# Five unused tiles that move the matmul operands of a two-block network by 64 to 320 bytes in SBUF

## The chip, the cores and the metric

The kernel runs on one core of one Trainium2 chip. The metric is the device time of one execution in microseconds (us); smaller is better. The kernel before takes 2571.19 us, the median of three runs between 2569.83 and 2571.62.

## The reference

Two network blocks run one after the other on a sequence of 512 tokens of width 1024, in fp32.

```
x1 = x + g_a * token_mixer(modulate(rmsnorm(x)), modulate(rmsnorm(ctx)))   # block 1
x2 = x1 + g_f * expert_choice_ffn(modulate(rmsnorm(x1)))                   # 16 experts
x3 = rmsnorm(x2)
h  = x3 + concat(pool_mixer, deltanet)(rmsnorm(x3) @ w_in) @ w_out         # block 2
h  = h + cross_attention(rmsnorm(h), mem)
h  = h + relu(rmsnorm(h) @ w_up)**2 @ w_down
out = rmsnorm(h)
```

The token mixer holds three branches: a gated linear recurrence with 8 heads, a gated convolution of width 3, and attention with 16 query heads. Nearly all the arithmetic is in products of a feature matrix (512 x 1024, or 256 x 1024 for the context) with a weights matrix.

## The kernel before, in words

**A product in three matmuls.** Weights arrive in `raw` tiles of 128 x 8 x 256 values by SyncE's DMA queue (`wload`). ScalarE rounds them into a high part `wh`, and VectorE takes the rest into a low part `wl` (`wsplit`, L111 and L112). Features are held in the same way as a high and a low tile. A product is then high x high, high x low and low x high, three matmuls in the type fp32r for each of the eight blocks of 128 rows. There are two forms:

- `lin_steps` (L120 to L128): the weights are the stationary operand, 128 columns of them, and the features stream past as the moving operand, 512 columns wide (256 for the context, for the memory and in two places that work in halves). L125 and L126 use `wh`, L127 uses `wl`.
- `lin_n` (L139 to L147): the features are the stationary operand, 128 tokens of them, and 256 columns of weights stream past. L145 and L147 stream `wh`, L146 streams `wl`.

```
self.nc.tensor.matmul(ps, a, xa, start=k == 0, stop=False)       # L125: a = weights, xa = features
self.nc.tensor.matmul(ps, xa, a, start=start and k == 0, ...)    # L145: the roles exchanged
```

Each matmul loads its stationary operand anew; the profile counts as many weight loads (PEld) as matmuls.

**Where the tiles lie.** SBUF is shared out by pools that stand like two stacks in each partition: a pool on the left side takes the next addresses upward, one on the right side the next addresses downward, and a release gives them back. `build` (L1424) makes all pools in order. A tile's address is thus the sum of the sizes of what stands before it. `wh` and `wl` stand at the start of the left stack, just above the constants, for the whole program: at 48,416, 56,608, 64,800 and 72,992 bytes, each with the remainder 32 modulo 256. The features stand in these tiles, with their first addresses in the built program:

| tile | holds | product it enters | address | modulo 256 |
|---|---|---|---|---|
| `hx` | normed tokens, block 1 | moving 512 (recurrence, gates, convolution); stationary (values, keys, queries) | 196,576 | 224 |
| `hc` | normed context | moving 256; stationary | 97,568 | 32 |
| `br`, `ao` | a branch's output | moving 512 (`merge`); `br` also stationary (`out_proj`) | 163,808 | 224 |
| `mT` | normed memory | moving 256; stationary (`mem_kv`) | 196,576 | 224 |
| `hn` | normed tokens entering block 2 | moving 512 | 97,568 | 32 |
| `y2`, `xo` | mixer's output, cross attention's output | stationary (`add_lin`) | 97,568 | 32 |
| `hxh`, `hxl` | normed tokens, cross attention and MLP | moving 512 (first group: in halves of 256) | 196,576 | 224 |
| `mh`, `ml` | MLP's hidden units | stationary (second half of `mlp`) | 120,736 | 160 |

In every one of these tiles the slices that matmuls read begin at multiples of 512 bytes from the tile's start, and the slices of `wh` and `wl` do as well, so one remainder holds for all slices of a tile.

**What sets the order.** Instructions are recorded in program order, with a priority for the weights' split, and a wait is put wherever a tile's data or its buffer is not yet there. Each engine takes its instructions in that order. The experts in between (`expert_pair`, L871) stream 201 MB of weights that come straight from memory, in plain fp32, and use no split.

Of the kernel before, what the change touches and what calls it, by code (L numbers as in the profile page):

```python
# [6 lines left out]
FT = mybir.dt.float32  # L7
# [71 lines left out]
class Net:  # L79
# [1344 lines left out]
    def build(self):  # L1424
        tc = self.tc
        P = lambda name, side="right", **kw: tc.alloc_tile_pool(name=name, bufs=1, side=side, reuse_waits="tile", **kw)
# [2 lines left out]

        self.xp = P("aT", "left")  # L1430
        self.aT = self.xp.tile([128, KK, S], FT, name="aT", tag="x")
        self.hcp = P("hctx", "left")
        self.hc = [[self.hcp.tile([128, C], FR, name=f"hc{p}{k}") for k in range(KK)] for p in "hl"]
        self.lpx = P("granule")
        self.lp = P("long")
        hx = [(self.lpx if i == 2 else self.lp).tile([128, 4, S], FR, name="hx", tag=f"hx{i}") for i in range(4)]
# [114 lines left out]
                self.pool_group(hd + 1)  # L1551
        self.hnp.release()
        self.y2p = P("y2", "left")
        self.y2 = self.hl(self.y2p, "y2", S)
        for k in range(4):
            self.split(self.y2[0][k], self.y2[1][k], self.ypool[:, k])
# [12 lines left out]
        self.dump("x3", self.x1)  # L1569
        self.y2p.release()  # L1570
        self.ap = P("cross", "left")
        self.xo = self.hl(self.ap, "xo", S)
        self.cross()
        self.hn = hl2()
# [1 line left out]
        nt.release()  # L1576
        self.ap.release()
        self.dump("x4", self.x1)
        self.ap = P("mlp")
        self.mlp()  # L1580
        self.ap.release()
        self.hnp.release()
        self.pp.release()
        self.xp.release()
        self.wp.release()
# [37 lines left out]
```

## Time and profile before

| | us |
|---|---|
| median of three runs | 2571.19 |
| the profiled execution, in all | 2567.61 |
| its span in the profile | 2565.8 |
| TensorE (PE) busy | 2468.1 |
| VectorE (DVE) busy | 1225.4 |
| ScalarE (ACT) busy | 992.6 |
| mean granted clock of TensorE | 0.992 |

The profile's time of one matmul is not what a matmul costs in a stream: matmuls overlap, and the profile models their ends. A row of the timeline has a start, and the distance between the starts of two matmuls, divided by the number of matmuls from one to the other, is the cost of one in that stream. The rows below are used in that way. [...]

In program order the span holds: norms and modulation (to 50 us), the recurrence's heads (50 to 500), merge, keys, convolution (to 860), queries and attention (to 1130), merge, memory, output projection and routing (to 1270), experts (to 1760), block 2's input products and delta solve (to 2010), its output projection, cross attention and MLP (to the end).

### The profile page before, as it was taken

Reading aid. Unit: us, or ns where it says so; the run is one execution under the profiler, and the core shown is the slowest. Engines: PE = TensorE matmul, PEld = TensorE weight load, DVE = VectorE, ACT = ScalarE, POOL = GpSimd, SP = SyncE. Lnnn points to the kernel's source line nnn. Section 1 sums busy time; section 2 is a strip of 40 time slices with the busy share of each in tenths; the row PEclk is TensorE's granted clock in tenths of the full one; section 3 lists DMA queues with packets and bytes.
Section 4 is the critical chain, followed back from the end, with each engine's and each line's share of the span. In section 5 each row is a group of like instructions: output and inputs, shape, how many; then the busy total and the mean of one; then the engine's idle time right before and its main releaser. Section 6 shows DMA issues by size and latency. Waiting matters only on the chain.

```text
span 2565.8 us, 34426 instructions
## 1 busy us (share of the span) xinstructions
PE 2468.1 (96%) x14348; PEld 1875.9 (73%) x14348; DVE 1225.4 (48%) x1960; ACT 992.6 (39%) x1665; POOL 100.0 (4%) x124
## 2 busy tenths in 40 slices
PE   6999999999999999999999999998999999999998
PEld 4888888689888886679833333334778989889898
DVE  4557575734443565544522222225884464532433
ACT  4446444542233466644321111114664444431332
POOL 0000000000001110010100000000000010000000
PEclk9999999999999999999999999998999999999999
DMA  8233222422323220044899999995220132223321
GB/s 276 66 83 99 83 67 66 140 91 83 99 83 98 84 81 1 1 149 156 295 406 409 409 409 410 409 409 185 66 82 17 34 99 66 91 83 99 99 99 50
DMA packets 244220, 386.85 MB, mean 151 GB/s; under 512 B 6864, under 2 KB 189136, under 8 KB 244064
## 3 DMA queue, kind: packets, MB, share of 16 engines
q1 hardware_dynamic: 238784, 365.98, 40.4%
q0 software_dynamic: 4704, 16.57, 1.8%
q8 instruction: 113, 1.85, 0.3%
q10 hardware_dynamic: 576, 2.10, 0.2%
q14 instruction: 43, 0.35, 0.0%
HBM read 376.23 MB, written 6.29 MB: 149 GB/s over the span
## 4 chain that ended last, share of the span: by engine, by line
PE 83%; DMA 7%; DVE 5%; ACT 4%; issue 1%; POOL 0%; SPq 0%; POOLq 0%; ACTq 0%; DVEq 0%
PE lin L125 11%; PE lin L126 11%; PE lin L127 11%; PE pair L871 11%; PE lin L145 6%; PE lin L147 6%; PE lin L146 6%; DMA ew<-in_w_up 4%; PE oT L717 2%; PE lps L383 2%; PE s L690 2%; DMA ew<-in_w_down 1%; PE ptp L704 1%; PE sps L953 1%; PE dzp L1239 1%
## 5 line engine op out<-in xcount | busy, mean ns | idle before, releaser
L112 DVE TENSOR_TENSOR wl<-raw,wh 128x1024 fp32r<-128x1024 f32 (+1 forms) x262 | 312.3, 1227 | 215.8 <-ACT wh L111 212.8
L111 ACT CAST wh<-raw 128x1024 fp32r<-128x1024 f32 (+1 forms) x262 | 258.5, 1028 | 404.3 <-PE lin L126 251.4
L871 PE MATMUL pair<-ew,XT 128*64 128x512 f32 x1024 | 259.0, 598 | 11.5 <-DMA ew<-in_w_up 11.4
L127 PE MATMUL lin<-hx,wl 128*128 128x512 f32 x576 | 231.4, 402 | 0.0
L125 PE MATMUL lin<-hx,wh 128*128 128x512 f32 x576 | 229.8, 399 | 0.0
L126 PE MATMUL lin<-hx,wh 128*128 128x512 f32 x576 | 227.9, 396 | 0.0
L871 PEld LDWEIGHTS pair<-ew,XT 128*64 128x64 f32 x1024 | 81.4, 136 | 167.0 <-issue 133.3
L145 PE MATMUL lin<-wh,mh 128*128 128x256 f32 x512 | 145.0, 283 | 0.0
L147 PE MATMUL lin<-wh,ml 128*128 128x256 f32 x512 | 144.7, 283 | 0.0
L146 PE MATMUL lin<-wl,mh 128*128 128x256 f32 x512 | 144.0, 281 | 0.0
L871 PE MATMUL pair<-ew,hT 128*64 128x512 f32 x512 | 138.4, 599 | 1.9 <-DMA ew<-in_w_down 1.9
L125 PE MATMUL lin<-hxh,wh 128*128 128x512 f32 (+1 forms) x352 | 131.7, 376 | 1.0 <-ACT hxh L972 0.9
L126 PE MATMUL lin<-hxl,wh 128*128 128x512 f32 (+1 forms) x352 | 131.9, 375 | 0.1
L127 PE MATMUL lin<-hxh,wl 128*128 128x512 f32 (+1 forms) x352 | 131.5, 375 | 0.0
L127 PEld LDWEIGHTS lin<-hx,wl 128*128 128x128 f32 x576 | 108.3, 188 | 25.7 <-issue 1.0
L125 PEld LDWEIGHTS lin<-hx,wh 128*128 128x128 f32 x576 | 108.4, 188 | 24.6 <-issue 1.2
L126 PEld LDWEIGHTS lin<-hx,wh 128*128 128x128 f32 x576 | 108.3, 188 | 24.7 <-issue 0.2
L871 PEld LDWEIGHTS pair<-ew,hT 128*64 128x64 f32 x512 | 44.7, 136 | 76.2 <-issue 67.0
L146 PEld LDWEIGHTS lin<-wl,mh 128*128 128x128 f32 x512 | 96.8, 189 | 0.1
L145 PEld LDWEIGHTS lin<-wh,mh 128*128 128x128 f32 x512 | 96.6, 189 | 0.1
L147 PEld LDWEIGHTS lin<-wh,ml 128*128 128x128 f32 x512 | 96.3, 188 | 0.0
L145 PE MATMUL lin<-wh,hx 128*128 128x256 f32 x320 | 91.2, 285 | 0.4 <-DVE sig L499 0.4
(547 smaller groups left out, 5423.9 us busy)
## 6 DMA issues: line engine op xcount, KB each, us to landing
ew<-in_w_gate SPq DMA_DIRECT2D x64, 1024.0 KB, 19.4
ew<-in_w_up SPq DMA_DIRECT2D x64, 1024.0 KB, 18.6
ew<-in_w_down SPq DMA_DIRECT2D x64, 1024.0 KB, 18.9
raw<-in_w_in SPq DMA_DIRECT2D x34, 1024.0 KB, 5.0
raw<-in_w_in SPq DMA_DIRECT2D x52, 512.0 KB, 5.3
raw<-in_ada_w SPq DMA_DIRECT2D x24, 1024.0 KB, 7.1
raw<-in_w_up SPq DMA_DIRECT2D x16, 1024.0 KB, 5.4
raw<-in_w_down SPq DMA_DIRECT2D x16, 1024.0 KB, 5.0
```

What stands on the lines that cost most here:

```text
L111: nc.scalar.copy(wh[:, a:a + 4, :n], raw[:, a:a + 4, :n])
L112: nc.vector.tensor_sub(wl[:, a:a + 4, :n], raw[:, a:a + 4, :n], wh[:, a:a + 4, :n].bitcast(FT))
L125: self.nc.tensor.matmul(ps, a, xa, start=k == 0, stop=False)
L126: self.nc.tensor.matmul(ps, a, xb, start=False, stop=False)
L127: self.nc.tensor.matmul(ps, b, xa, start=False, stop=k == KK - 1)
L145: self.nc.tensor.matmul(ps, xa, a, start=start and k == 0, stop=False)
L146: self.nc.tensor.matmul(ps, xa, b, start=False, stop=False)
L147: self.nc.tensor.matmul(ps, xb, a, start=False, stop=stop and k == KK - 1)
L383: nc.tensor.matmul(ps[:, c].rearrange("p (b h x) -> p b h x", h=2, x=m), Xc[:, c], Y[:, c * n4:(c + 1) * n4], start=True, stop=True)
L690: nc.tensor.matmul(s[:, a:b], qT[2 * pair + hh][:, 128 * t:128 * t + 128], kT[p][:, a:b], start=p == 0, stop=p == 1)
L717: self.nc.tensor.matmul(self.oT[64 * hh:64 * hh + 64], self.vn[:, kt, 64 * g:64 * g + 64], PT[kt // 2][:, 2 * (kt % 2) + hh], start=kt == ...
L871: self.nc.tensor.matmul(ps[j][64 * e:64 * e + 64], lhs[:, k0 + k, 64 * e:64 * e + 64], w[e][:, k, 512 * j:512 * j + 512], start=k0 + k == ...
```

## The change

Five tiles are allocated that nothing reads or writes: two of 192 bytes a partition, two of 64 and one of 128. Three stand at the bottom of left pools that are later released (`hctx`, `y2` and `cross`), and two have right pools of their own: `gap`, which stands under everything on the right side for the whole program, and `gapm`, under the MLP's pool.

```
         self.hcp = P("hctx", "left")
+        self.hcp.tile([128, 48], FT, name="gap")
         self.hc = [[self.hcp.tile([128, C], FR, name=f"hc{p}{k}") for k in range(KK)] for p in "hl"]
+        gap = P("gap")
+        gap.tile([128, 48], FT, name="gap2")
         self.lpx = P("granule")
...
         self.y2p = P("y2", "left")
+        self.y2p.tile([128, 16], FT, name="gap3")
         self.y2 = self.hl(self.y2p, "y2", S)
...
         self.ap = P("cross", "left")
+        self.ap.tile([128, 16], FT, name="gap4")
         self.xo = self.hl(self.ap, "xo", S)
...
+        gap2 = P("gapm")
+        gap2.tile([128, 32], FT, name="gap5")
         self.ap = P("mlp")
         self.mlp()
         self.ap.release()
+        gap2.release()
         self.hnp.release()
+        gap.release()
```

No engine's instructions change their order, their shapes or their number: the two built programs hold the same 18,012 instructions, and one wait differs (a GpSimd fill of the convolution's padding waits for a matmul three places earlier). What changes is addresses. The weights' tiles and the constants stay. Of the remainders modulo 256:

| tile | before | after | features minus weights, before | after |
|---|---|---|---|---|
| `wh`, `wl` | 32 | 32 | | |
| `hx`, `br`, `ao`, `mT`, `hxh`, `hxl` | 224 | 32 | 192 | 0 |
| `hc` | 32 | 224 | 0 | 192 |
| `hn` | 32 | 32 | 0 | 0 |
| `y2`, `xo` | 32 | 96 | 0 | 64 |
| `mh`, `ml` | 160 | 96 | 128 | 64 |

Working tiles of the right side move along by 192 bytes (the recurrence's, the delta rule's), and so do some of the attention's (`qT`, from 224 to 32) but not its keys `kT`. Every shift is a multiple of 64 bytes. The experts' tiles stay, except for one buffer of weights that moves from 224 to 32.

## Rows read from the trace of the kernel before

**Rows 1.** The page: engines' busy time, and the chain by engine.
```profile
PE 2468.1 (96%) x14348; PEld 1875.9 (73%) x14348; DVE 1225.4 (48%) x1960; ACT 992.6 (39%) x1665; POOL 100.0 (4%) x124
PE 83%; DMA 7%; DVE 5%; ACT 4%; issue 1%; POOL 0%; SPq 0%; POOLq 0%; ACTq 0%; DVEq 0%
```
**Rows 2.** Busy time by stretch: us, engines (instructions), granted clock, DMA share, GB/s.
```profile
50.00:500.00 450.00, 443.94 (x2957) 378.81 (x2955) 284.53 (x443) 216.78 (x308) 0.00 (x0) 1.00 0.29 86
...
1300.00:1750.00 450.00, 428.88 (x1737) 158.37 (x1733) 112.89 (x214) 57.68 (x99) 6.65 (x7) 1.00 1.02 406
...
2010.00:2566.00 556.00, 542.53 (x3613) 491.85 (x3612) 236.54 (x376) 189.96 (x350) 11.15 (x17) 1.00 0.26 83
```
**Rows 3.** PE's waits: us in total, times, longest; first row and later one.
```profile
PE plat L287 <- DVE xn L269: 15.8, 2, 14.9
...
PE lin L145 <- ACT wh L111: 1.0, 1, 1.0
```
**Rows 4.** Groups of PE matmuls by form: shapes, count, busy us, mean ns, idle.
```profile
L125 PE MATMUL lin<-hx,wh 128*128 128x512 f32 x576 | 229.8, 399 | 0.0
...
L145 PE MATMUL lin<-wh,mh 128*128 128x256 f32 x512 | 145.0, 283 | 0.0
...
L125 PE MATMUL lin<-hxh,wh 128*128 128x512 f32 x288 | 114.2, 397 | 0.0
...
L145 PE MATMUL lin<-wh,hx 128*128 128x256 f32 x320 | 91.2, 285 | 0.4 <-DVE sig L499 0.4
...
L125 PE MATMUL lin<-brh,wh 128*128 128x512 f32 x128 | 50.7, 396 | 0.7 <-DVE sig L164 0.7
...
L145 PE MATMUL lin<-wh,y2h 128*128 128x256 f32 x128 | 36.8, 288 | 1.3 <-ACT y2h L440 1.3
```
**Rows 5.** Timeline of PE (start us, us): `hx` moving, 623 matmuls apart.
```profile
619.35 0.39 PE L125 MATMUL lin<-hx,wh 128*128 128x512 f32 x1
...
764.71 0.39 PE L127 MATMUL lin<-hx,wl 128*128 128x512 f32 x1
```
**Rows 6.** Timeline: `hn` moving, 79 matmuls apart.
```profile
1787.39 0.39 PE L125 MATMUL lin<-hnh,wh 128*128 128x512 f32 x1
...
1805.33 0.39 PE L126 MATMUL lin<-hnl,wh 128*128 128x512 f32 x1
```
**Rows 7.** Timeline: `hc` stationary, 47 apart; then `hx` stationary, 95 apart.
```profile
602.71 0.28 PE L145 MATMUL lin<-wh,hch 128*128 128x256 f32 x1
...
608.35 0.28 PE L147 MATMUL lin<-wh,hcl 128*128 128x256 f32 x1
608.47 0.28 PE L145 MATMUL lin<-wh,hx 128*128 128x256 f32 x1
...
619.24 0.28 PE L147 MATMUL lin<-wh,hx 128*128 128x256 f32 x1
```
**Rows 8.** Timeline: `hx` stationary later, 47 apart.
```profile
856.77 0.28 PE L145 MATMUL lin<-wh,hx 128*128 128x256 f32 x1
...
862.31 0.28 PE L147 MATMUL lin<-wh,hx 128*128 128x256 f32 x1
```
**Rows 9.** Timeline: `y2` stationary, 328 apart.
```profile
2019.57 0.28 PE L146 MATMUL lin<-wl,y2h 128*128 128x256 f32 x1
...
2058.93 0.28 PE L146 MATMUL lin<-wl,y2h 128*128 128x256 f32 x1
```
**Rows 10.** Timeline: `mT` moving, 47 apart.
```profile
1245.49 0.28 PE L125 MATMUL lin<-mT,wh 128*128 128x256 f32 x1
...
1250.83 0.28 PE L127 MATMUL lin<-mT,wl 128*128 128x256 f32 x1
```
**Rows 11.** Timeline: `mh` and `ml` stationary, 505 apart.
```profile
2490.03 0.28 PE L146 MATMUL lin<-wl,mh 128*128 128x256 f32 x1
...
2549.96 0.28 PE L147 MATMUL lin<-wh,ml 128*128 128x256 f32 x1
```

More of the change, by code (lines that the diff above doesn't have):

```diff
@@ L1432, in build @@
         self.hcp = P("hctx", "left")
+        self.hcp.tile([128, 48], FT, name="gap")
         self.hc = [[self.hcp.tile([128, C], FR, name=f"hc{p}{k}") for k in range(KK)] for p in "hl"]
+        gap = P("gap")
+        gap.tile([128, 48], FT, name="gap2")
         self.lpx = P("granule")
@@ L1553, in build @@
         self.y2p = P("y2", "left")
+        self.y2p.tile([128, 16], FT, name="gap3")
         self.y2 = self.hl(self.y2p, "y2", S)
@@ L1571, in build @@
         self.ap = P("cross", "left")
+        self.ap.tile([128, 16], FT, name="gap4")
         self.xo = self.hl(self.ap, "xo", S)
@@ L1578, in build @@
         self.dump("x4", self.x1)
+        gap2 = P("gapm")
+        gap2.tile([128, 32], FT, name="gap5")
         self.ap = P("mlp")
@@ L1581, in build @@
         self.ap.release()
+        gap2.release()
         self.hnp.release()
+        gap.release()
         self.pp.release()
```

## The prediction

> **What bounds the kernel now.** I read the profile's page first: TensorE is busy for 96% of the span, and 83% of the chain that ends last is PE [rows 1]. Then the busy time by stretch. From 50 to 500 us and from 2010 us to the end TensorE is busy 99% and 98% of the time at the full granted clock, while VectorE stands at 63% and 43%; only the experts, 1300 to 1750 us, are held by DMA, which is in use all the time at 406 GB/s [rows 2]. Then PE's waits: the longest is the start-up wait for the first normed tokens, 15.8 us, and a wait for split weights, the thing that would starve the products, comes to 1.0 us [rows 3]. So outside the experts and the delta rule's solve the time is a sum over matmuls, and what counts is the distance from one start to the next, which the mean in a group's row (399 ns and so on, [rows 4]) does not show. That distance is read from the timeline, as last start minus first, divided by the number between.
>
> **What the timeline says about places.** With the granted clock at 1.00 and no wait in between:
> - 512 columns moving, features at remainder 224 (`hx`): 145.36 us over 623, 233.3 ns [rows 5].
> - 512 columns moving, features at remainder 32, as the weights (`hn`): 17.94 us over 79, 227.1 ns [rows 6]. Shape, type and weights' tiles are the same, 6.2 ns less.
> - 256 columns of weights moving, features stationary at 32 (`hc`): 5.64 us over 47, 120.0 ns. The very next stream has the same weights tile moving and `hx`, at 224, stationary: 10.77 us over 95, 113.4 ns [rows 7]. Later the same pair runs at 5.54 over 47, 117.9 ns [rows 8]. So the pair 32/224 has two levels, and I take their middle, 115.6.
> - `y2` stationary at 32: 39.36 us over 328, again 120.0 ns [rows 9].
> - `mh` and `ml` stationary at 160: 59.93 us over 505, 118.7 ns [rows 11].
> - 256 columns of features moving at 224 (`mT`): 5.34 us over 47, 113.6 ns [rows 10].
>
> A cost thus goes with the difference of the two operands' remainders, and with opposite signs: with 512 columns equal remainders are the cheap case, with 256 they are the dear one. The reading is that the stream of moving columns and the load of the next stationary operand, which run at the same time, get in each other's way at some distances.
>
> [...]
>
> **The change part by part.** The instructions and their order stay, so no work is added and no queue is passed; the terms are counts times differences. Each count is that of a group's row, times three for its three lines.
> 1. 512 columns moving, 224 to 32: `hx` 576 x 3, `hxh` 288 x 3, `br` 128 x 3 [rows 4], and attention's output `ao` and the gates that fill attention (`fill`), by their loops 64 x 3 each: 3360 matmuls, each 6.2 ns less: -20.8 us.
> 2. Features stationary, 224 to 32: `hx` 320 x 3 [rows 4], `br` in `out_proj` (by its loops 384), `mT` (192): 1536 matmuls from 115.6 to 120.0: +6.8 us.
> 3. 256 columns of features moving: `mT` 192 and the halves of `hxh` 192 go from 224 to 32; `hc`, 384, goes from 32 to 224. Equal counts exchange places, so this is 0, whatever the price.
> 4. `hc` stationary, 32 to 224: 288 matmuls, 120.0 to 115.6: -1.3 us.
> 5. `y2` and `xo` stationary, 32 to 96: 128 x 3 [rows 4] each, 768. The trace holds no steady stream with the weights moving at 32 and the stationary operand at 96. The nearest row is `mT` moving at 224 with the weights stationary at 32, the same distance of 64 from moving to stationary: 113.6 [rows 10]. Bounds: 113.4 from below (the cheapest stream with 256 columns, rows 7), and from above 122.4, one more step of 4.5 ns (from 113.4 to 117.9, rows 7 and 8) over 117.9; that is a loss. I take 115.6, because a pair that shows a low level elsewhere shows a high one too. 768 x -4.4 = -3.4 us, between -5.1 and +1.8.
> 6. `mh` and `ml` stationary, 160 to 96: 512 x 3 = 1536 [rows 4], from 118.7 to the same 115.6: -4.8 us, between -8.1 and +5.7.
> 7. The rest: the recurrence's and the delta rule's plain fp32 matmuls move along with their partners, and the expert buffer lies in the stretch that DMA holds; 0. If attention's scores (`qT` goes to 32, `kT` stays) change by as much as a step, 256 matmuls x 4.5 ns is 1.2 us either way.
>
> Sum: -20.8 + 6.8 - 1.3 - 3.4 - 4.8 = -23.5 us. Not all of it need reach the end. In the recurrence (50 to 500 us) the chain of a head runs through VectorE and ScalarE, and VectorE is busy 63% there; the net of its share is about -6 us (768 of term 1, 384 `hx` and 192 `hc` stationary, and 384 `hc` moving that gain while their counterparts lie elsewhere), of which I take a quarter to be lost in those waits: +1.5. In the last 556 us VectorE has room (43%), weights come at 83 GB/s where the experts draw 406, and I take nothing off. That leaves -22.0 us. On the profiled execution, 2567.6 us with a span of 2565.8, that gives 2545.6; it is 3.6 us below the median of the runs, so on the median it is 2571.2 - 22.0 = 2549.2.
>
> **The rivals.**
> 1. Region, not remainder: no change. The cheap 512 stream (`hn`) lies at 97,568 to 130,336 bytes and the dear ones at 163,808 and above; `hc` and `y2` lie in the same low part and `hx` and `mT` high. Any cause that goes with the region, or with the stage, fits these rows as well, and no tile moves by more than 320 bytes. Against it: `mh` and `ml` stretch from 120,736 to about 194,000, through both parts, and their price lies between the two and not at 120.0 in one part and 115.6 in the other; and a region that makes 512 columns cheaper and 256 dearer is odd (though so is a remainder). 2571, within 2 us.
> 2. The new pair 32/96 gains nothing: terms 5 and 6 at 120.0, which is 0 and +2.0 in place of -8.2: 2549.2 + 10.2 = 2559.4. For it: distances of 0 and 128 both cost about 119 to 120, and the only stream at a distance of 64 has the roles exchanged. Against it: term 3's streams at that distance are the cheapest there are.
> 3. Slower: remainders rule only the streams with 256 columns, where the load takes as long as the stream, and `hn`'s 227.1 comes from its region. Then term 1 is 0, terms 2 and 4 stay (+5.5), and terms 5 and 6 decide: at 120.0 they make +2.0, in all +7.5, 2578.7; at the upper bound +7.5, in all +13.0, 2584. It counts as slower from 119.0 ns on for the new pair. For it: all the matmuls at 227 ns are from one stage. Against: the streams of rows 5 and 6 share shape, type, weights' tiles and clock.
> 4. The gain is lost to other engines: matmuls that come sooner meet splits that are not done. If all of the recurrence's share is lost, 4.5 us more: 2554. Against: 1.0 us of waits for the split [rows 3].
>
> **How the numbers follow.** The forecast 0.65, rival 1 0.09, rival 2 0.14, rival 3 0.06, rival 4 0.06. What measurement of this kernel can tell from no change is about 0.2%, 5 us. Faster: 0.65 + 0.14 + 0.06 = 0.85; same 0.09; slower 0.06. The forecast's own range goes with the bounds of terms 5 and 6: at the low price they gain 5.0 us more, and with nothing lost in the recurrence 1.5 more, so 2542.7; some 2 us below that for a term 2 that stays at a low level, 2541. On the other side, rival 2 at 2559.4 and half-way to the upper bound of the unknown pair (another 2.7) gives 2562. Rivals 1 and 3 are left out, with a little of the rest. The single time is 2549.
>
> **What would show it.** In the profile after: the stream of rows 5 at 227 ns; that of rows 6 unchanged; `hx` stationary at 120 where it was 113 and 118; `y2`, `xo`, `mh` and `ml` between 113 and 118. From the end backward, the last 556 us would be shorter by 864 matmuls of `hxh` x 6.2 ns and by terms 5 and 6, less 1 us for the halves, together about 12 us; the stretch of the experts would keep its length. It is wrong if rows 5's stream stays at 233 (rivals 1 or 3), or if streams change as said and the stretches do not shorten (rival 4).

## The result, and the profile after

| | us |
|---|---|
| changed kernel, median of 4 runs | 2541.24 (2539.28 to 2543.25) |
| kernel before, 4 runs in the same session | 2571.38 (2569.83 to 2571.62) |
| ratio | 0.9886, 95% interval 0.9873 to 0.9900 |
| profiled execution after, in all | 2539.76 (before 2567.61) |
| its span | 2537.4 (before 2565.8) |

The change takes 30 us off the median; the forecast was 22. The direction and the cause were right. The gain was undersized by about a quarter, and the median lies only 0.24 us above the bottom of the stated range, 2541.

The page after, first the engines' busy time and then the chain that ended last. They answer to [rows 1].

```profile
PE 2440.5 (96%) x14348; PEld 1867.7 (74%) x14348; DVE 1223.7 (48%) x1960; ACT 992.6 (39%) x1665; POOL 101.1 (4%) x124
...
PE 50%; DMA 6%; DVE 4%; ACT 2%; issue 1%; POOL 0%; POOLq 0%; ACTq 0%; DVEq 0%
```

TensorE is busy 27.6 us less with the same 14,348 matmul records, and the span fell by 28.4; no other engine's busy time changed by more than 2 us. The shares of the chain (50% where it was 83%) are no finding: the chain traced here accounts for only 63% of the span, so its shares can't be set against those of before.

The busy time by stretch, with the columns of [rows 2]. The last stretch ends 28 us sooner than there.

```profile
50.00:500.00 450.00, 443.66 (x2974) 380.82 (x2974) 286.96 (x451) 220.02 (x314) 0.00 (x0) 1.00 0.30 88
1300.00:1750.00 450.00, 427.61 (x1718) 158.37 (x1716) 119.30 (x223) 61.22 (x106) 7.75 (x9) 0.99 1.01 401
2010.00:2538.00 528.00, 515.94 (x3566) 473.14 (x3564) 229.39 (x364) 182.28 (x336) 11.16 (x17) 0.99 0.27 87
```

The granted clock is 0.99 to 1.00 in these stretches and 0.989 over the span (0.992 before), no higher than before, so it gave nothing. The two waits of TensorE that [rows 3] shows read the same after the change:

```profile
PE plat L287 <- DVE xn L269: 15.8, 2, 14.9
...
PE lin L145 <- ACT wh L111: 1.0, 1, 1.0
```

What changed is the distance from one matmul's start to the next. The timeline after, for each stream its first and last matmul: `hx` moving with 512 columns (623 apart, answering to [rows 5]), `hn` moving (79, [rows 6]), `hc` and then `hx` stationary (47 and 95, [rows 7]), `mT` moving (47, [rows 10]), `y2` and `xo` stationary (328 and 299, [rows 9]), and `mh` and `ml` stationary, in the MLP's first and in its second half (767 each; [rows 11] is a part of the second).

```profile
613.59 0.40 PE L125 MATMUL lin<-hx,wh 128*128 128x512 f32 x1
...
754.83 0.39 PE L127 MATMUL lin<-hx,wl 128*128 128x512 f32 x1
...
1778.60 0.39 PE L125 MATMUL lin<-hnh,wh 128*128 128x512 f32 x1
...
1796.51 0.39 PE L126 MATMUL lin<-hnl,wh 128*128 128x512 f32 x1
...
596.63 0.28 PE L145 MATMUL lin<-wh,hch 128*128 128x256 f32 x1
...
601.96 0.28 PE L147 MATMUL lin<-wh,hcl 128*128 128x256 f32 x1
602.07 0.28 PE L145 MATMUL lin<-wh,hx 128*128 128x256 f32 x1
...
613.47 0.28 PE L147 MATMUL lin<-wh,hx 128*128 128x256 f32 x1
...
1234.92 0.28 PE L125 MATMUL lin<-mT,wh 128*128 128x256 f32 x1
...
1240.56 0.28 PE L127 MATMUL lin<-mT,wl 128*128 128x256 f32 x1
...
2008.91 0.28 PE L146 MATMUL lin<-wl,y2h 128*128 128x256 f32 x1
...
2046.14 0.28 PE L146 MATMUL lin<-wl,y2h 128*128 128x256 f32 x1
...
2137.36 0.28 PE L146 MATMUL lin<-wl,xoh 128*128 128x256 f32 x1
...
2171.27 0.28 PE L146 MATMUL lin<-wl,xoh 128*128 128x256 f32 x1
...
2268.66 0.28 PE L145 MATMUL lin<-wh,mh 128*128 128x256 f32 x1
...
2355.83 0.28 PE L147 MATMUL lin<-wh,ml 128*128 128x256 f32 x1
...
2443.01 0.28 PE L145 MATMUL lin<-wh,mh 128*128 128x256 f32 x1
...
2530.17 0.28 PE L147 MATMUL lin<-wh,ml 128*128 128x256 f32 x1
```

Last start minus first, divided by the number apart, in ns:

| stream | features minus weights, before and after | ns before | ns after |
|---|---|---|---|
| `hx` moving, 512 | 192, 0 | 233.3 | 226.7 |
| `hn` moving, 512 (not moved) | 0, 0 | 227.1 | 226.7 |
| `hc` stationary | 0, 192 | 120.0 | 113.4 |
| `hx` stationary | 192, 0 | 113.4 | 120.0 |
| `mT` moving, 256 | 192, 0 | 113.6 | 120.0 |
| `y2`, `xo` stationary | 0, 64 | 120.0 (`y2`) | 113.5, 113.4 |
| `mh`, `ml` stationary, second half | 128, 64 | 118.7 | 113.6 |

`hc` and `hx` have exchanged their prices along with their places: the same pair of streams, in the same order, at the same time of the program.

### The profile page after: what moved, and what is told of

Read it like the earlier page. It is cut to its first block, busy times and chain, and to the rows that moved or that the text cites. A ratio compares the mean times of both kernels' runs of the same rounds, so it can differ in the third digit from the quotient of the medians.

```text
span 2537.4 us, 34426 instructions
## 1 busy us (share of the span) xinstructions
PE 2440.5 (96%) x14348; PEld 1867.7 (74%) x14348; DVE 1223.7 (48%) x1960; ACT 992.6 (39%) x1665; POOL 101.1 (4%) x124
## 4 chain that ended last, share of the span: by engine, by line
PE 50%; DMA 6%; DVE 4%; ACT 2%; issue 1%; POOL 0%; POOLq 0%; ACTq 0%; DVEq 0%
PE pair L871 11%; PE lin L125 5%; PE lin L126 5%; PE lin L127 5%; PE lin L147 4%; PE lin L145 4%; PE lin L146 4%; DMA ew<-in_w_up 4%; PE oT L717 2%; PE s L690 2%; DMA ew<-in_w_down 1%; PE ptp L704 1%; PE sps L953 1%; PE dyp L1235 1%; PE dzp L1239 1%
## 5 line engine op out<-in xcount | busy, mean ns | idle before, releaser
L125 PE MATMUL lin<-hx,wh 128*128 128x512 f32 x576 | 226.6, 393 | 0.0
L126 PE MATMUL lin<-hx,wh 128*128 128x512 f32 x576 | 224.9, 390 | 0.0
```

Of the source, the lines that this page charges most:

```text
L126: self.nc.tensor.matmul(ps, a, xb, start=False, stop=False)
```

## The experiments

All the kernels below that compute the network, except e6, are the kernel before with other tiles added; a tile of n values shifts what stands after it by 4n bytes. Ratios are to the kernel before, timed in the same session. "By term" means that for each of the 14,348 matmul records the distance from its start to the next start is set against the same distance in the profile of the kernel before, and the differences are summed by what the matmuls read. A wait behind a matmul is thus counted with it; e2 shows how far a term can be trusted.

**e1: is it the features' own place, or the difference?** The weights' tiles move from 32 to 224 and the features that matter stay at 224.

```
+        cp.tile([128, 48], FT, name="gapw")
         self.wp = tc.alloc_tile_pool(name="weights", bufs=1, side="left")
```

> 192 unused bytes ahead of the weights' pool in the kernel before: the weights go to the remainder 224, hx, br, ao, mT, hxh stay at 224, hc, hn, y2, xo go along with the weights to 224, mh and ml stay at 160. Differences (features minus weights): 0 for all but mh and ml, 192 for these. If the difference of the remainders decides: hx moving with 512 columns goes from 233.3 to about 226.7 ns, hx stationary to 120.0, hn stays at 227, mh and ml go from 119 to 113 to 118; in all -22 (512) +5 (stationary) +2 (memory and halves moving) -5 (mh, ml) = about -20 us, 2551. If the features' own remainder decides (32 is the good place for 512 columns): hx stays at 233, hn gets 6 ns dearer (456 matmuls, +3 us), y2, xo and hc stationary get cheaper (about -5 us); 2571 within 4 us.

Measured: 2553.35 us against 2569.76, ratio 0.9936 (0.9919 to 0.9952). The stream of `hx`, 623 apart, with the features where they had been:

```profile
615.28 0.40 PE L125 MATMUL lin<-hx,wh 128*128 128x512 f32 x1
...
756.52 0.39 PE L127 MATMUL lin<-hx,wl 128*128 128x512 f32 x1
```

That is 226.7 ns at remainder 224, where [rows 5] had 233.3 at 224. `hx` stationary stood at 120.0, and `y2`, which moved along with the weights, stayed at 120.0. It is the difference of the two operands, not a place of their own. `mh` and `ml`, at a difference of 192 here, run at 117.8. By term e1 has -19.7 us from the 512 columns, +4.1 from the stationary features and -2.3 from `mh` and `ml`, where the expectation had -22, +5 and -5; so it came out 2 us above the 2551 expected.

**e3 and e4: the two halves of the change.** e3 moves the right side alone (terms 1 and 2), e4 the left side and the MLP's tiles alone (terms 4 to 6). The releases of the pools are left out here.

```
e3:  gap = P("gap"); gap.tile([128, 48], FT, name="gap2")
     gap2 = P("gapm"); gap2.tile([128, 16], FT, name="gap5")
e4:  self.hcp.tile([128, 48], FT, name="gap")
     self.y2p.tile([128, 16], FT, name="gap3")
     self.ap.tile([128, 16], FT, name="gap4")
     gap2 = P("gapm"); gap2.tile([128, 16], FT, name="gap5")
```

> Of the change only the pad under the right side's stack (hx, br, ao, mT, hxh, hxl and qT go from 224 to 32); mh and ml are brought back to 160, hc, y2, xo stay at 32. Theory (prices are those of the streams by difference, and they add up): 3360 x -6.6 = -22 for 512 columns, +5 for the stationary ones, +2 for memory and halves that move with 256 columns, +1 for attention's scores: -14 us, 2557. Rival (the gain comes from somewhere else, the end of the program for example): under -7 us or over -22.

> The other part of the change alone: hc goes to 224, y2 and xo to 96, mh and ml to 96; hx, br, ao, mT, hxh stay at 224. Theory: y2, xo 768 x -6.5 = -5, mh, ml 1536 x -5.7 = -8.7, hc stationary -1, hc moving -2: -16 us, 2555, and with the right side's part it adds up to the whole change's -30 within 2 us. Rival (the two parts hide each other): the sum of the two parts differs from the whole by more than 4 us.

Measured: e3 2555.39 us, ratio 0.9941 (0.9925 to 0.9958); e4 2557.27, ratio 0.9956 (0.9944 to 0.9969). By term, e3 has -19.6 us from the 512 columns and +4.4 from the stationary features, and +1.8 from the scores (on these see e2); e4 has -3.9 from `y2` and `xo`, -5.5 from `mh` and `ml`, and -0.1 from the 512 columns. e4 gained 12.5 us between the medians, less than its expected 16. The two ratios multiply to 0.9897, where the whole change has 0.9886: 2.8 us apart, not quite the 2 us expected, and within the intervals. In the profiles the two parts make -22.9 us together, and the whole -28.3. Of these 5.5 us `mh` and `ml` account for 4.2: their second half ran at 120.0 ns in e3, at a difference that e3 does not change, and at 117.8 in e4. One more thing in e4 fits no term: `hx` stationary, at the difference it had before, ran at 117.8 ns (95 apart) where [rows 7] shows 113.4:

```profile
609.24 0.28 PE L145 MATMUL lin<-wh,hx 128*128 128x256 f32 x1
...
620.43 0.28 PE L147 MATMUL lin<-wh,hx 128*128 128x256 f32 x1
```

In all `hx` stationary cost 1.25 us more there without having been touched.

**e2: the control.** The right side moves by 256 bytes, which changes every address and no remainder.

```
+        gap = P("gap"); gap.tile([128, 64], FT, name="gap2")
```

> The kernel before with 256 unused bytes under the right side's stack: every tile there moves, and no remainder modulo 256 changes. Theory (only the remainder modulo 256 counts): every stream as before, hx 233.3 ns, 2570 within 3 us. Rival (the period is longer, or any other place helps): streams of hx change by 2 ns or more, the time by 5 us or more.

Measured: 2569.03 us, ratio 0.9995 (0.9985 to 1.0005). `hx` moving, 623 apart, is 233.3 ns as before:

```profile
619.29 0.39 PE L125 MATMUL lin<-hx,wh 128*128 128x512 f32 x1
...
764.65 0.39 PE L127 MATMUL lin<-hx,wl 128*128 128x512 f32 x1
```

Terms 1, 5 and 6 are zero to 0.01 us. The control also tells how much of a table by term is noise: attention's scores come out at +1.0 us, the first product of block 2 at -1.8 and the memory's halves at +1.8, with no remainder changed. The reason is TensorE's granted clock, which drops at slightly different times in each execution. The same eight scores, in the kernel before, in the control and in the changed kernel (stretch, its length, TensorE's busy time, granted clock, DMA share, GB/s):

```profile
949.60:951.10 1.50, 1.50 (x8) 1.00 0.41 89
...
949.32:952.03 2.71, 2.71 (x8) 0.50 0.70 246
...
937.33:940.05 2.72, 2.72 (x8) 0.50 0.65 206
```

At a granted clock of 0.50 they take 1.2 us longer (2.71 and 2.72 us against 1.50), whatever the remainders. The memory's halves show the same: twelve of them stand 0.21 us apart in the control and 0.11 before. In the first product of block 2 it is the kernel before that starts at 0.50: from 1773.90 to 1777.10 us its matmuls of 256 columns stand 0.21 us apart there, and 0.12 from 1777.62 on, at 1.00.

**m1: all distances, by themselves.** A kernel that holds only streams of 72 matmuls of one kind, each kind at eight differences, with the weights at two remainders (x: 128, y: 192).

```
def moving(name, n, d, base, reps):        # "wide": n = 512, "half": n = 256
    ...
    nc.tensor.matmul(o, a, xa, ...); nc.tensor.matmul(o, a, xb, ...); nc.tensor.matmul(o, b, xa, ...)
for base, mark in ((0, "x"), (64, "y")):
    for d in DISTS:                        # 0, 32, ... 224
        moving(f"wide{d:03d}{mark}", 512, (base + d) % 256, base, 3)
```

> Not the network: streams of 72 fp32r matmuls by themselves, in the same three products, with random weights and features, for eight differences (features minus weights, 0 to 224 in steps of 32), in the three forms: features moving with 512 columns (wide), with 256 (half), features stationary under 256 columns of weights (stat); once with the weights at remainder 128 (x) and once at 192 (y). The output holds nothing of the reference. If the difference alone decides, x and y give the same price at each difference, wide is 227 at 0 and 233 at 192, half 120 at 0 and 113 to 118 at 192, stat 120 at 0, 113.5 at 64, 119 at 128, 113 to 118 at 192. If something of the network (other engines' traffic, the place in SBUF) makes the prices, all differences cost the same within 1 ns here.

Measured, ns from start to start (x; y is the same to 0.4):

| features minus weights | 0 | 32 | 64 | 96 | 128 | 160 | 192 | 224 |
|---|---|---|---|---|---|---|---|---|
| 512 moving | 226.8 | 233.4 | 229.0 | 233.3 | 233.3 | 234.3 | 233.3 | 233.2 |
| 256 moving | 119.8 | 117.8 | 117.8 | 119.9 | 118.6 | 117.3 | 113.5 | 118.2 |
| features stationary | 119.9 | 118.3 | 117.7 | 118.7 | 118.6 | 120.0 | 117.8 | 116.7 |

Two streams of it in the timeline, from the fourth matmul to the last (68 apart): 512 columns at difference 0, then at 192.

```profile
45.13 0.39 PE L50 MATMUL wide000x<-fh,wh 128*128 128x512 f32 x1
...
60.56 0.39 PE L52 MATMUL wide000x<-fh,wl 128*128 128x512 f32 x1
...
147.17 0.40 PE L50 MATMUL wide192x<-fh,wh 128*128 128x512 f32 x1
...
163.03 0.40 PE L52 MATMUL wide192x<-fh,wl 128*128 128x512 f32 x1
```

15.43 and 15.86 us over 68 are 226.9 and 233.2 ns, with nothing else running on the core that the streams wait for. So neither the network's stage nor its region is needed for it. Plain fp32 matmuls of 256 columns, which the profile shows as two records each (48 for the 24 that the kernel issues), ran at 215.8 ns a record at 0, 64, 128 and 192 alike; the effect was seen in fp32r only, and plain fp32 was tried at no other place or width. But 64 with the features stationary is 117.7, where the changed kernel ran `y2` at 113.5.

**e5: another difference for the right side.** Its gap is 128 bytes in place of 192, so that `hx` and its like stand at 64 from the weights; the rest is the changed kernel.

```
-        gap.tile([128, 48], FT, name="gap2")
+        gap.tile([128, 32], FT, name="gap2")
...
-        gap2.tile([128, 32], FT, name="gap5")
+        gap2.tile([128, 48], FT, name="gap5")
```

> The whole change, but the pad under the right side is 128 bytes in place of 192 (and the MLP's 192 in place of 128): hx, br, ao, mT, hxh lie at 96, a difference of 64 to the weights; hc, y2, xo, mh, ml lie as in the change. The streams by themselves gave 229.0 ns at 64 for 512 columns against 226.8 at 0, and for features stationary 117.7 (113.4 in the network) against 120.0. Theory: 3360 x +2.2 = +7.4, 1536 stationary x -2.3 to -6.6 = -3.5 to -10, halves -0.8: between +3 and -4 us against the change, 2538 to 2545, and the stream of hx with 512 columns at 229. Rival (only a difference of 0 is cheap for 512 columns in the network): hx at 233, and +12 us or more against the change.

Measured: 2545.54 us, ratio 0.9898 (0.9880 to 0.9916). `hx` moving, 623 apart, then `y2` stationary, 322 apart:

```profile
614.29 0.39 PE L125 MATMUL lin<-hx,wh 128*128 128x512 f32 x1
...
756.89 0.39 PE L127 MATMUL lin<-hx,wl 128*128 128x512 f32 x1
...
2010.04 0.28 PE L145 MATMUL lin<-wh,y2h 128*128 128x256 f32 x1
...
2047.97 0.28 PE L146 MATMUL lin<-wl,y2h 128*128 128x256 f32 x1
```

228.9 ns is what the streams by themselves had said for 64 (229.0), and not the rival's 233. Term 1 is -13.5 us and term 2 turns from +4.8 to -1.7; the trade between them is about even. The time is just above the 2538 to 2545 expected and 4 us above the changed kernel's in the same session (a1), a step that the intervals of the two ratios do not separate. `y2`, at the difference and the addresses that it has in the changed kernel, runs at 117.8 here and 113.5 there. A pair thus has two levels, and the pair does not say which.

**m2: what sets the level?** The streams of 256 columns at 64 and 192 again, each behind five different predecessors (512 columns, stationary features, halves, plain fp32, or a pause), and the whole twice.

```
before(mark); stationary(f"stat{d:03d}{mark}", d, 0, 3)
before(mark); moving(f"half{d:03d}{mark}", 256, d, 0, 3)
```

> Not the network: streams of 72 fp32r matmuls by themselves, at the differences 64 and 192, features stationary (stat) or moving with 256 columns (half), each right behind another kind of work: w 512 columns at difference 0, s features stationary at 0, h 256 columns moving at 0, p plain fp32 matmuls, g a wait for VectorE. The output holds nothing of the reference. Question: what picks the level of 113.5 or of 117.8 ns at one and the same difference. If the work just before does (the phase in which the stream begins), one and the same stream shows both levels in this run, and each the same in both repetitions; in the network stat at 64 had 113.4 behind 512 columns (w) and stat at 192 had 113.3 behind stationary features at 0 (s), 117.8 behind w. If the level belongs to the stream (its addresses above 256 bytes), each shows one level whatever precedes it: stat at 64 and at 192 117.7, half at 64 117.8, half at 192 113.5, as in the run with all differences.

Measured: stationary at 64 ran at 117.8 ns behind 512 columns (w) and at 113.4 to 113.5 behind stationary features (s), halves and plain fp32. Behind a pause (g) it ran at 113.4 in the first round and at 117.8 in the second. The four streams, 68 apart each:

```profile
51.34 0.28 PE L61 MATMUL stat064w<-wh,fh 128*128 128x256 f32 x1
...
59.35 0.28 PE L63 MATMUL stat064w<-wh,fl 128*128 128x256 f32 x1
...
106.52 0.28 PE L61 MATMUL stat064s<-wh,fh 128*128 128x256 f32 x1
...
114.24 0.28 PE L63 MATMUL stat064s<-wh,fl 128*128 128x256 f32 x1
...
248.81 0.28 PE L61 MATMUL stat064g<-wh,fh 128*128 128x256 f32 x1
...
256.52 0.28 PE L63 MATMUL stat064g<-wh,fl 128*128 128x256 f32 x1
...
488.73 0.28 PE L61 MATMUL stat064g<-wh,fh 128*128 128x256 f32 x1
...
496.74 0.28 PE L63 MATMUL stat064g<-wh,fl 128*128 128x256 f32 x1
```

8.01 us against 7.72 and 7.71. In this run the kind of work before goes with the level, in both rounds alike, except behind a pause, where it isn't repeatable. In the network that is not enough: `y2` in e5 stands behind the same instructions as in the changed kernel and has the other level. My guess of which predecessor gives which level was wrong: for stationary at 64 behind w it had 113.4 ns, and 117.8 was measured.

**a1: the changed kernel once more,** with no edit.

> The change itself once more, on the same chip as the others: 2541 within 3 us, a ratio of 0.987 to 0.990.

Measured: 2541.39 us, ratio 0.9884 (0.9864 to 0.9905). In this execution the MLP's first half ran at the low level again (113.6 ns), its second, 767 apart, at the high one:

```profile
2441.24 0.28 PE L145 MATMUL lin<-wh,mh 128*128 128x256 f32 x1
...
2531.60 0.28 PE L147 MATMUL lin<-wh,ml 128*128 128x256 f32 x1
```

90.36 us where the other execution of the same kernel took 87.16: 117.8 against 113.6 ns, 3.2 us from one draw of the level. The draw does not fall only at the stream's start. In both executions the second half begins with 47 distances of about 117.8 ns, and then one is longer, 140 ns in the first profile and 135 in a1. Behind it the first profile goes on at 113.3 and a1 at 117.8. These are the two matmuls on either side of it in the first profile, whose stream began at 2443.01 and ended at 2530.17:

```profile
2448.54 0.30 PE L147 MATMUL lin<-wh,ml 128*128 128x256 f32 x1
2448.68 0.28 PE L145 MATMUL lin<-wh,mh 128*128 128x256 f32 x1
```

In the nine profiles of the network, a stretch of 30 or more matmuls of one product, with 256 columns and no distance over 130 ns, keeps one level, apart from its first few: 113.3, 117.8, 118.7 or 120.0 ns in the profile of the kernel before, and 113.3, 117.8 or 120.0 in the first one of the changed kernel. What makes the longer distance stays open. The runs of the changed kernel spread over 2537.16 to 2543.5. Several draws can make that, and so can the clock: over the 32 runs of the kernel before that are on record beside the experiments, the time goes with the mean granted clock, from 2563.91 us at 0.995 to 2576.51 at 0.986, about 1.1 us for each 0.001 by a line through them. How the two share in the changed kernel's spread was not measured run by run.

**m3: is there a better place?** The streams of m1 at 17 finer differences.

```
for d in (0, 4, 8, 16, 24, 40, 48, 56, 72, 80, 112, 144, 208, 232, 240, 248, 252):
```

> Not the network: the streams of the run with all differences once more, at differences that are no multiples of 32 bytes, and at 0 as a tie to it (wide, half, stat as there, weights at remainder 128). The output holds nothing of the reference. If the cost comes from lines of 32 or 64 bytes that both streams want at once, differences between 0 and 32 cost 512 columns a value between 226.8 and 233.4, and steps of 4 bytes do little. If a better place than a multiple of 32 exists, some difference lies below 225 ns for 512 columns or below 113 ns for 256, and a kernel can be made that uses it.

Measured for 512 columns: 226.8 ns at 0, and between 230.7 (at 252) and 238.0 (at 4) elsewhere. With 256 columns, features stationary range from 115.6 (8) to 120.0, moving halves from 113.7 (112) to 126.5 (8). For 512 columns nothing tried beats equality, and a misplacement by a single value costs 11 ns. That is against the idea of lines of 32 or 64 bytes, by which steps of 4 bytes would have done little and 512 columns would have stayed within 233.4 ns. Difference 4, 68 apart (16.18 us; difference 0 is at 226.8 here as in m1):

```profile
80.05 0.41 PE L50 MATMUL wide004x<-fh,wh 128*128 128x512 f32 x1
...
96.23 0.40 PE L52 MATMUL wide004x<-fh,wl 128*128 128x512 f32 x1
```

**e6: each product its own difference.** On top of the change, `wh` starts 192 bytes later in the products that have `hx`, `br` or `mT` stationary, and 64 later for the halves. `wh` alone is placed apart, and three tiles that had two buffers have one, to make room for it.

```
+    def wsplit(self, raw, n=256, off=0):
+        wh = self.wp.tile([128, KK * 256 + 64], FR, ...)[:, off:off + KK * 256]...
...
+            w = self.wsplit(self.wload(W, c0), off=48)
```

> The changed kernel, and beside it: the high weights tile wh is placed 192 bytes later in those products where the features are stationary and stood at difference 0 (hx, br, mT), and 64 bytes later in those where features move in halves of 256 columns (mT, and the first group of hxh); wl stays where it was for want of room, and mpart, qn and of have one buffer in place of two to make some. Theory (a matmul's spacing goes with the difference of its own two operands modulo 256 bytes, and every product can have its own difference): two thirds of the 1536 stationary matmuls leave the 120.0 ns of difference 0 for 117.8 or 113.3, 1024 x (-2.2 to -6.7) = -2.3 to -6.9 us; two thirds of the 384 halves gain 0.6 to 1.6 us; two thirds of the 288 with hc stationary lose 0.4 to 1.3 us, since that tile now meets wh at difference 0. Together -1.6 to -8 us against the changed kernel at 2541.4: 2533 to 2540, with hx 512 still at 226.7 ns. Rival (the matmuls of one product take turns between wh and wl, and the dearer of the two differences sets the pace of both): no gain, 2541. A loss, above 2543, would be the price of the single buffers, and would show as waits of PE on them.

Measured: 2541.04 us (2536.25 to 2545.35), ratio 0.9895 (0.9877 to 0.9913): no difference from the change that the runs can tell. In its trace `hx` stationary, 95 apart, is at 117.8 ns where the change has 120.0, though one matmul in three still meets `wl` at difference 0:

```profile
603.11 0.28 PE L145 MATMUL lin<-wh,hx 128*128 128x256 f32 x1
...
614.30 0.28 PE L147 MATMUL lin<-wh,hx 128*128 128x256 f32 x1
```

In this stream the distance behind those that meet `wl` stays at 120.0 ns, and the other two have 117.2 and 116.2, so each matmul has about the price of its own two operands. Term 2 falls by 2.5 us and `hc` costs 0.5 more, against the change's first profile. The halves of `mT` rose by 1.5, because 16 of them fell on a drop of the clock (about 0.21 us apart; granted clock 0.86 from 1250 to 1260 us). The rival (no gain, because the dearer of the two sets the pace) is refuted in the stream, and the theory's gain came out at its small end, below what these runs resolve.

## Why the prediction was right, and where it was too small

By term, from two profiled executions of the changed kernel, each against the profiled execution before:

| term | forecast | first profile | a1 |
|---|---|---|---|
| 1: 512 columns moving | -20.8 | -19.5 | -19.5 |
| 2: `hx`, `br`, `mT` stationary | +6.8 | +4.8 | +4.9 |
| 3: 256 columns moving | 0 | -1.2 | -1.5 |
| 4: `hc` stationary | -1.3 | -0.9 | -0.2 |
| 5: `y2`, `xo` | -3.4 | -4.0 | -4.0 |
| 6: `mh`, `ml` | -4.8 | -8.7 | -5.5 |
| 7: scores | 0 | +1.2 | +1.1 |
| all other matmuls | 0 | 0.0 | -2.2 |
| lost in the recurrence | +1.5 | in the terms | in the terms |
| sum | -22.0 | -28.3 | -26.7 |

The forecast of term 7 is 0, with up to 1.2 either way. The +1.2 and +1.1 are no cost of the places: they are the eight scores at the granted clock of 0.50, shown under e2. The -2.2 of all other matmuls in a1 is mostly the first product of block 2, which did not fall on that clock there.

- **The mechanism** stood up: the distance of the two operands modulo 256 bytes. e1 shows that it is the difference (226.7 ns with the features left at 224), e2 that the period divides 256 (233.3 ns before and after), m1 that it needs neither this kernel nor this stage (226.8 and 233.3 ns). Rival 1 (the region) and rival 3 (its claim that 512 columns don't care) fall with the 226.7 ns in the changed kernel and in e1. The reading beneath it, that the moving stream and the next load get in each other's way, was only argued: that the plain fp32 streams of m1 showed no difference (215.8 ns a record) is a fact it doesn't account for. The trace before shows that weight loads run beneath the matmuls: PEld is busy for 59.00 of the 59 us from 2490 to 2549 (`mh` and `ml`, 256 columns) and for 116.00 of the 144 from 620 to 764 (`hx`, 512 columns). It does not show that the two hinder each other.
- **Term 6 was mis-sized, twice.** I took 118.7 ns for all 1536 matmuls from a stretch in the MLP's second half. The first half, which I did not read, runs at 120.0 before the change: 92.04 us over 767, in these rows of the kernel before.

```profile
2285.72 0.28 PE L145 MATMUL lin<-wh,mh 128*128 128x256 f32 x1
...
2377.76 0.28 PE L147 MATMUL lin<-wh,ml 128*128 128x256 f32 x1
```

  So the mean to start from was 119.3. And the price after was taken as 115.6, the middle of two levels; a long stream has one or the other for most of its length. Both halves drew 113.6 in the first profile (-8.7 us) and one of them in a1 (-5.5).
- **Term 5** is the same: 113.4 for all 768 in place of the middle, -4.0 us, and -1.4 in e5, where both streams drew 117.8. Rival 2 (the new pair gains nothing) is wrong; even the high level gains 2.2 ns.
- **Term 2** was right in its price after (119.9 to 120.0 in each of its streams once begun) and too high in size, by the price before: `br`'s four streams all stood at the high level then (117.8 ns), so its 384 matmuls lost 2.2 ns each in the streams and not 4.4.
- **Term 1** has 226.7 in the streams, 0.4 below the forecast, but its 3360 matmuls gained 5.8 ns on average and not 6.2. In the recurrence 657 of 788, those with one of their kind before and after, gained 5.6 each, and 131 at the border to other work gained nothing. A count times a stream's price overstates short products.
- **Term 3's zero** came out as a small gain. Moving at 192, `hc` stands at 114.2, 117.7 or 118.8 in its streams of 24 and gained 1.5 us, near its count times 4.4 ns (1.7). `mT` and `hxh` went up to 120.0 in their streams, but the distances of all their 384 matmuls together rose by 0.2 only, as waits among them became shorter (one behind `mT` from 2.23 to 1.45 us).
- **The recurrence** shortened by 4.3 us from 50 to 500 in the first profile, near the forecast of 6 less 1.5. The reason given was wrong: no wait of VectorE took it (distances over 300 ns for 512 columns, over 160 else, changed by 0.3 us in all); what term 1 lacks there is mostly the matmuls at the borders. Rival 4 did not occur.
- **From the end backward** I expected about 12 us in the last 556; it was 17.7 in the first profile, and terms 5 and 6 are most of the excess. The experts' matmuls kept their time (0.0 us).
- **The range** held by 0.24 us. The forecast reached 2541 with 2 us for a term 2 that stays at a low level. That did not happen, as its streams all rose to 120.0; term 2 is smaller by 2.0 us in the first profile for another reason, the price before. That the two sizes agree is luck.

What stays open: what in the chip depends on the difference, why 0 is best for 512 columns and among the dearest with 256, and what sets a stream's level at its start and behind a longer distance. Why the median moved by 30 us and the two profiles by 28 and 27 is also not settled; each profile is one execution, and draws of the level (3.2 us) and the mean granted clock (0.992 before, 0.989 and 0.992 after) make differences of that size.

## What to carry to other kernels

Where TensorE is busy all the time and its matmuls are fp32r with a fresh stationary operand each, read the distance from start to start in a long stream; if one shape has several prices at the same granted clock, list the operands' addresses modulo 256 bytes before looking for a wait. An unused tile of 64 to 192 bytes is then a cheap edit, and it should be chosen for the widest and most frequent product first: here 512 columns at difference 0 were worth 20 us, and all else together 9. A profile of one execution does not rank versions that differ by less than a draw of the level or a drop of the clock, here 3.2 us and 1.0 to 1.8. Read every stage's streams, since the same tiles had 120.0 ns in one half of the MLP and 118.7 in the other.

## What the runs showed of the hardware that was not expected

- The spacing of fp32r matmuls with 128 x 128 stationary operands depends on the difference of the two operands' addresses modulo 256 bytes: 226.8 ns at 0 and 229.0 to 238.0 at all other differences tried, for 512 columns; 113.4 to 126.5 ns for 256, where 0 costs 119.8 to 120.0.
- A difference of one fp32 value (4 bytes) is the worst place found for 512 columns: 238.0 ns, 5% over equality.
- With the features stationary, a stream of 256 columns at a difference of 64 or 192 has two levels, 113.4 and 117.8 ns, drawn at its start and again behind a longer distance (135 to 140 ns in the MLP's second half), and kept in between; one kernel can show either in two executions (a1), 3.2 us apart over 767 matmuls. A difference of 128 has shown two prices as well, 118.7 and 120.0 (e3 and the kernel before).
- Plain fp32 matmuls were indifferent: 215.8 ns a record, two records each, for 256 columns at the four differences tried.
- The times at which the granted clock drops to 0.50 differ between executions of the same instructions, and change what a table by term says of a product by 1.0 to 1.8 us (the control, e2).
